# A convolution's last taps during attention: from multiplies and accumulating transfers to two GpSimd instructions per tap

## The chip, the cores and the metric

The kernel runs on one core of a Trainium2 chip. A core has five engines that run their own instruction streams and meet at semaphores: TensorE (PE in the profile, with its weight loads as PEld), VectorE (DVE), ScalarE (ACT), GpSimd (POOL) and SyncE (SP), which here only issues transfers. Transfers (DMA) run on 16 engines of their own; they are issued from SyncE's queue and from GpSimd's. The metric is the device time of one execution in microseconds (us), the median over several runs.

## The reference

Two layers of an encoder on a sequence of 1024 tokens with 1024 channels, then a final RMSNorm. In each layer a normalized input is projected once, and two things are computed from it side by side: attention with 8 heads, and a depthwise convolution of 31 taps on 512 channels. Both go through one output matrix; a gated feed-forward part follows.

```python
h = _rmsnorm(x, g_mix[l])
p = h @ w_in[l]
...                                   # queries, keys and values from p
y_attn = _mla_attention(q_nope, q_rope, k_nope, k_rope, v)
a, gt = jnp.split(p[..., o3:], 2, axis=-1)
u = a * jax.nn.sigmoid(gt)
u = _dwconv(u, w_dw_conv[l], b_dw_conv[l])          # 31 taps for each channel
u = jax.nn.silu(_layernorm(u, g_conv_ln[l], b_conv_ln[l]))
y = jnp.concatenate([y_attn, u], axis=-1) @ w_o[l]
x = x + y
...                                   # gated feed-forward part with a 3-tap convolution
```

The change concerns the line with `_dwconv`: for each channel c and time s it adds up 31 products w[t, c] * u[s + t - 15, c].

## The kernel before, in words

Channels lie on the 128 partitions and the 1024 tokens along the free dimension, so the convolution's 512 channels are four tiles of 128x1024, with j from 0 to 3. Its input tile is called gate in the profile (`u[j]`, which is made in place), its sum is `conv[j]`, and a tap's weight is a column of the parameter tile `par`, one number for each partition. A tap is a multiply of a shifted `u[j]` by that column, and an add into `conv[j]`.

The four sums are begun in the projections (`project`): ScalarE makes the middle tap with the bias, VectorE adds 12 to 16 taps for each j (L1734), and some taps go by ScalarE and an accumulating transfer (`tap_far`, L1740 and L1741). What is left, 50 taps in the first layer and 48 in the second, is called late and is done in `attention`.

Attention works in 64 steps, for 8 heads of 8 query tiles. In each step TensorE computes scores for two steps ahead (L1536, six matmuls of 512 columns), turns the probabilities of earlier tiles by eight transposes (L1565), and multiplies them with the values (L1588, four matmuls). VectorE finds the row maximum of the scores (L1538) and makes the low part of the turned probabilities (L1568), ScalarE takes the exponential (L1546) and casts the turned tiles (L1567).

The order of each engine's instructions is the order in which the program emits them; nothing reorders them. Work beside the steps is put on an agenda, a list of functions for each step, which run when that step has been emitted. GpSimd's stream in attention holds the following:

- the late taps, which the agenda spreads over the first 56 steps in proportion to planned costs (`LATE_COST`, `SIDE_TIME`);
- for every second head a multiply of the head pair's output `yt` by the inverse sums (L1614, agenda steps 23, 39 and 55), and five or four steps later the low half of that output (`ys`, L206), whose upper half is cast by ScalarE (L204);
- at step 55 four transfers that fetch parts of the output matrix (`wo`, L869). From step 58 on ScalarE negates each of them (L185) and GpSimd issues the accumulating transfer that completes it (L186);
- from step 60 on three adds that sum the four `conv[j]` into `lns` (L1762), for the layer norm's mean, which TensorE begins with (`lnp`, L1778).

A late tap has one of three kinds, in a pattern of five (`LATE_KINDS`), the first row for the first half of the taps and the second row for the second half:

- act: ScalarE multiplies in two halves (L1748, one half in each of two steps), and a transfer that GpSimd issues adds the product to `conv[j]` (L1756);
- pool: GpSimd multiplies by the tap, broadcast along the free dimension as a second tensor (L1751), and a transfer adds the product (L1756);
- both: GpSimd multiplies in the same way and adds by an instruction of its own (L1754).

The first layer has 30 taps of kind pool, 10 of kind both and 10 of kind act; the second has 29, 10 and 9. A tile for a product comes from a pool of 31 slots of 128x1024 that is shared with most other tiles (`blk`).

Of the kernel before, what the change touches and what calls it, by code (L numbers as in the profile page):

```python
# [12 lines left out]
AF = mybir.ActivationFunctionType  # L13
ALU = mybir.AluOpType
AX = mybir.AxisListType

T = 1024
# [55 lines left out]
ROW_LATE = {0: (6,)}  # L73
E = mybir.EngineType
MANUAL = [E.PE, E.DVE, E.Activation, E.Pool]
LATE_KINDS = (("pool", "both", "act", "pool", "act"), ("pool", "both", "pool", "pool", "pool"))
LATE_COST = {"act": 1.1, "pool": 3.5, "both": 4.8}
NEAR_TAPS = (12, 14, 16, 14)
NEAR_ORDER = (0, 1, 2, 3)
FAR_TOGETHER = 3  # L80
# [41 lines left out]
class Encoder:  # L122
# [1379 lines left out]
    def attention(self, l, u, conv, away, spill, kvs, loaded, ahead, wo, begun):  # L1502
# [147 lines left out]
        while any(rest.values()):  # L1650
            j = max((j for j in rest if rest[j]), key=lambda j: (all(j != e for e, _ in late[-2:]), len(rest[j]), -j))
            late.append((j, rest[j].pop(0)))
        kinds = [LATE_KINDS[2 * i // len(late)][i % 5] for i in range(len(late))]
        costs, taken = [LATE_COST[kind] for kind in kinds], set()
        for i, (j, t) in enumerate(late):
# [87 lines left out]
    def tap_late(self, l, j, t, u, y, kind):  # L1743
        lo, hi, s = self.span(t)
        p = self.blk(f"late{l}_{j}_{t}")
        if kind == "act":
            for a, b in ((lo, T // 2), (T // 2, hi)):
                self.nc.scalar.activation(out=p[:, a:b], in_=u[:, a + s:b + s], func=AF.Copy, scale=self.tap(l, j, t))  # L1748
                yield
        else:  # L1750
            self.nc.gpsimd.tensor_tensor(out=p[:, lo:hi], in0=u[:, lo + s:hi + s],  # L1751
                                         in1=self.tap(l, j, t).broadcast_to([128, hi - lo]), op=ALU.mult)
        if kind == "both":
            self.nc.gpsimd.tensor_tensor(out=y[:, lo:hi], in0=y[:, lo:hi], in1=p[:, lo:hi], op=ALU.add)  # L1754
        else:
            self.nc.gpsimd.dma_start(out=y[:, lo:hi], in_=p[:, lo:hi], accum_op=ALU.add)  # L1756

    def conv_total(self, l, conv, j):
        if j == 1:
# [137 lines left out]
```

## Time and profile before

| What | Value |
|---|---|
| median of 3 runs | 2277.29 us |
| lowest and highest | 2277.22 and 2278.43 us |
| the profiled execution's own span | 2274.7 us |
| TensorE busy in that span | 2267.6 us |
| GpSimd busy in that span | 782.9 us |
| attention, first layer | about 199 to 405 us |
| attention, second layer | about 1328 to 1534 us |

The span runs from the first to the last instruction of the profiled execution; the device time of a run has some 2.6 us around it. Times in views are in us from the span's start, means of one instruction in ns. In rows of the groups stands: line, engine, operation, out<-in by tile names, shapes, count, then busy time and mean of one, then the engine's idle time just before and what ended it. In rows of the timeline stands: start, duration, engine, line, operation, tiles, count, and in brackets the idle time before. A GpSimd instruction that follows a transfer's issue is shown from before that issue has ended, so its shown duration is longer by up to 0.3 us than that of one that follows another instruction.

### The profile page before, as it was taken

The page shows a single profiled execution, that of the slowest core. Times are in us where ns is not written, and L with a number is a line of the kernel's source. Part 1 is how long each engine was busy: PE and PEld are TensorE (multiplying, and loading weights), DVE is VectorE, ACT ScalarE, POOL GpSimd, SP SyncE. Part 2 cuts the span into 40 slices and gives each one's busy share as a digit, 9 for nine tenths or more (in the row PEclk, how much of TensorE's full clock was granted, in tenths as well). Part 3 has the DMA queues.
Part 4 walks back from the last instruction along what each step waited for, and adds up shares of the span by engine and source line. Part 5 has one row for each costly group of instructions (what it writes and reads, how often), then busy time and mean ns, then how long its engine had stood idle before and what let it go on. Part 6 is the DMA issues. An engine that isn't in the chain of part 4 may idle for free.

```text
span 2274.7 us, 30503 instructions
## 1 busy us (share of the span) xinstructions
PE 2267.6 (100%) x10682; PEld 1888.4 (83%) x10682; DVE 1724.7 (76%) x2299; ACT 1286.8 (57%) x2050; POOL 782.9 (34%) x812
## 2 busy tenths in 40 slices
PE   9999999999999999999999999999999999999999
PEld 8888888888888888888888888888888888888888
DVE  7989888768877776776559788886697777768765
ACT  5355877646655555544523468774475555555444
POOL 1222788532333333001412237873323333320032
PEclk9999999999999999999999999999999999999999
DMA  6889998856899998935968999967669999988356
GB/s 192 166 182 266 195 199 182 215 153 139 208 283 300 272 298 203 336 103 146 205 137 167 218 253 201 184 150 211 173 131 230 272 299 283 287 216 315 104 120 173
DMA packets 199145, 475.73 MB, mean 209 GB/s; under 512 B 27232, under 2 KB 35280, under 8 KB 198992
## 3 DMA queue, kind: packets, MB, share of 16 engines
q0 software_dynamic: 103136, 222.46, 48.7%
q1 hardware_dynamic: 95568, 250.80, 33.0%
q8 instruction: 84, 1.38, 0.2%
q14 instruction: 69, 0.57, 0.1%
q10 hardware_dynamic: 288, 0.53, 0.1%
HBM read 309.29 MB, written 80.40 MB: 171 GB/s over the span
## 4 chain that ended last, share of the span: by engine, by line
PE 96%; DVE 1%; DMA 1%; issue 1%; ACT 0%; POOL 0%; DVEq 0%; POOLq 0%; ACTq 0%; SPq 0%
PE p L1095 35%; PE pd L1283 18%; PE s L1536 8%; PE po L906 6%; PE o L1588 5%; PE t L1565 5%; PE pq L222 3%; PE pa L222 3%; PE pkv L222 2%; PE pg L222 2%; PE pg L541 2%; PE pn L222 1%; PE pv L1514 1%; PE pk L222 1%; PE pa L541 1%
## 5 line engine op out<-in xcount | busy, mean ns | idle before, releaser
L1095 PE MATMUL p<-b,w 128*128 128x512 f32 x3552 | 806.7, 389 | 0.1
L1095 PEld LDWEIGHTS p<-b,w 128*128 128x128 f32 x3552 | 666.4, 188 | 139.7 <-DVE w L1474 1.1
L1283 PE MATMUL pd<-ab,wd 128*128 128x512 f32 (+1 forms) x1920 | 422.2, 381 | 0.0
L1283 PEld LDWEIGHTS pd<-ab,wd 128*128 128x128 f32 x1920 | 350.8, 188 | 69.4 <-DVE ab L1474 0.4
L186 POOL DMA_DIRECT2D w<-wu x96 | 84.8, 886 | 359.6 <-ACT w L185 317.9
L1536 PE MATMUL s<-k,q 96*128 96x512 f32 x768 | 207.6, 405 | 0.0
L1568 DVE TENSOR_TENSOR pt<-t,pt 128x512 fp32r<-128x512 f32 x256 | 165.1, 686 | 53.1 <-ACT pt L1567 51.8
L1751 POOL TENSOR_TENSOR late<-gate,par 128x1014 f32<-128x1014 f32 (+12 forms) x79 | 171.7, 2173 | 18.7 <-DMA qrd<-qr 18.7
L1567 ACT CAST pt<-t 128x512 fp32r<-128x512 f32 x256 | 137.8, 589 | 66.5 <-PE t L1565 62.8
L1486 DVE SCALAR_TENSOR_TENSOR o<-zg,par,o 128x1023 f32<-128x1023 f32 x88 | 112.8, 1283 | 75.4 <-ACT o L1480 74.0
L186 POOL DMA_DIRECT2D w<-in_w_up x116 | 100.5, 867 | 199.6 <-ACT w L185 181.2
L1538 DVE TENSOR_REDUCE mx<-s 128x1 f32<-128x1024 f32 x128 | 155.8, 1217 | 0.6 <-PE s L1536 0.6
L1536 PEld LDWEIGHTS s<-k,q 96*128 96x128 f32 x768 | 135.4, 189 | 23.1
L1546 ACT ACTIVATE p<-s,mx 128x1024 f32<-128x1024 f32 x128 | 144.8, 1131 | 1.8 <-DVE mx L1538 1.8
L1734 DVE SCALAR_TENSOR_TENSOR conv<-gate,par,conv 128x1009 f32<-128x1009 f32 (+7 forms) x112 | 142.3, 1274 | 3.7 <-ACT conv L603 1.0
L1588 PE MATMUL o<-pt,v 128*128 128x512 f32 x512 | 140.8, 398 | 0.0
L869 POOL DMA_DIRECT2D wd<-in_w_down x44 | 32.8, 749 | 307.8 <-PE pd L1283 306.7
L1044 DVE TENSOR_TENSOR zg<-p,zg 128x512 f32<-128x512 f32 x88 | 60.6, 690 | 99.7 <-PE p L1095 92.5
L1472 ACT CAST ab<-ac 128x512 fp32r<-128x512 f32 x130 | 80.1, 617 | 98.2 <-DVE ac L1218 95.5
L185 ACT ACTIVATE w<-w 128x512 fp32r<-128x512 f32 x212 | 133.4, 629 | 3.0
L1565 PEld LDWEIGHTS t<-ident,p 128*128 128x128 f32 x1024 | 119.9, 141 | 18.2 <-ACT p L1546 0.4
L1565 PE MATMUL t<-ident,p 128*128 128x128 f32 x1024 | 133.0, 273 | 0.0
(2105 smaller groups left out, 4110.1 us busy)
## 6 DMA issues: line engine op xcount, KB each, us to landing
w<-in_w_up POOLq DMA_DIRECT2D x232, 256.0 KB, 7.1
wu<-in_w_up SPq DMA_DIRECT2D x88, 512.0 KB, 5.7
w<-wu POOLq DMA_DIRECT2D x96, 256.0 KB, 5.6
sd<-in_w_down SPq DMA_DIRECT2D x44, 512.0 KB, 9.6
ws<-sd SPq DMA_DIRECT2D x44, 512.0 KB, 6.6
wd<-in_w_down POOLq DMA_DIRECT2D x88, 256.0 KB, 5.4
act<-v SPq DMA_DIRECT2D x36, 512.0 KB, 5.4
ac<-act SPq DMA_DIRECT2D x72, 256.0 KB, 6.0
```

What stands on the lines that cost most here:

```text
L186: self.nc.gpsimd.dma_start(out=lo, in_=src, accum_op=ALU.add)
L222: nc.tensor.matmul(ps[:, HALVES[c]], w, x[:, HALVES[c]], start=(k == 0 and s == 0), stop=(k == n - 1 and s == 2))
L1095: nc.tensor.matmul(ps, w[p][:, k * 128:(k + 1) * 128], b[:, q], start=(i in (1, 5, 2) and k == 0 and t == 0), stop=(k == 3 and t == 2), sk ...
L1283: nc.tensor.matmul(ps[t, m][:, cs], w[i, j][p][:, m * 128:(m + 1) * 128], b[:, q, cs], start=(i in (1, 5, 2) and j == 0 and s == 0), stop= ...
L1536: nc.tensor.matmul(ps[:, cs], q[i][0:96, qs], k[j][0:96, cs], start=(s == 0), stop=(s == 2))
L1538: nc.vector.tensor_reduce(out=mx, in_=ps, op=ALU.max, axis=AX.X, negate=True)
L1546: nc.scalar.activation(out=p, in_=ps, func=AF.Exp, bias=mx, accum_out=st["sums"][:, qt:qt + 1])
L1565: nc.tensor.transpose(tp[:, i, qi * 128:(qi + 1) * 128], st["p"][2 * qp + qi][:, kt * 128:(kt + 1) * 128], self.ident)
L1568: nc.vector.tensor_tensor(out=lo, in0=tp, in1=hi.bitcast(F32), op=ALU.subtract)
L1588: nc.tensor.matmul(po, v[2 * c + i][:, h // 2, e, :], pt[s][:, i, :], start=(c == 0 and i == 0 and s == 0), stop=(c == 3 and i == 1 and s ...
L1734: self.nc.vector.scalar_tensor_tensor(out=y[:, lo:hi], in0=u[:, lo + s:hi + s], scalar=self.tap(l, j, t), in1=y[:, lo:hi], op0=ALU.mult, o ...
L1751: self.nc.gpsimd.tensor_tensor(out=p[:, lo:hi], in0=u[:, lo + s:hi + s], in1=self.tap(l, j, t).broadcast_to([128, hi - lo]), op=ALU.mult)
```

## The change: two kinds of late taps in place of three

The kinds both and pool become one: GpSimd multiplies with the tap as a scalar operand (one tensor operand and a pointer to one number for each partition) and adds the product to `conv[j]` itself. Only the act taps still end in a transfer. The pattern keeps the act taps at the same places of the list, and the planned costs are replaced, so some taps move by a step on the agenda.

```diff
-LATE_KINDS = (("pool", "both", "act", "pool", "act"), ("pool", "both", "pool", "pool", "pool"))
-LATE_COST = {"act": 1.1, "pool": 3.5, "both": 4.8}
+LATE_KINDS = (("pool", "pool", "act", "pool", "act"), ("pool", "pool", "pool", "pool", "pool"))
+LATE_COST = {"act": 1.1, "pool": 3.6}
@@ def tap_late(self, l, j, t, u, y, kind):
         lo, hi, s = self.span(t)
         p = self.blk(f"late{l}_{j}_{t}")
-        if kind == "act":
-            for a, b in ((lo, T // 2), (T // 2, hi)):
-                self.nc.scalar.activation(out=p[:, a:b], in_=u[:, a + s:b + s], func=AF.Copy, scale=self.tap(l, j, t))
-                yield
-        else:
-            self.nc.gpsimd.tensor_tensor(out=p[:, lo:hi], in0=u[:, lo + s:hi + s],
-                                         in1=self.tap(l, j, t).broadcast_to([128, hi - lo]), op=ALU.mult)
-        if kind == "both":
+        if kind == "pool":
+            self.nc.gpsimd.tensor_scalar(out=p[:, lo:hi], in0=u[:, lo + s:hi + s], scalar1=self.tap(l, j, t), scalar2=None, op0=ALU.mult)
             self.nc.gpsimd.tensor_tensor(out=y[:, lo:hi], in0=y[:, lo:hi], in1=p[:, lo:hi], op=ALU.add)
-        else:
-            self.nc.gpsimd.dma_start(out=y[:, lo:hi], in_=p[:, lo:hi], accum_op=ALU.add)
+            return
+        for a, b in ((lo, T // 2), (T // 2, hi)):
+            self.nc.scalar.activation(out=p[:, a:b], in_=u[:, a + s:b + s], func=AF.Copy, scale=self.tap(l, j, t))
+            yield
+        self.nc.gpsimd.dma_start(out=y[:, lo:hi], in_=p[:, lo:hi], accum_op=ALU.add)
```

In the changed file the multiply is L1747, the add L1748, the transfer of an act tap L1753, the sums into `lns` L1759. The streams of TensorE, VectorE and SyncE hold the same instructions in the same order as before. ScalarE's holds the same instructions, with some of the late halves one step earlier.

## The prediction

> **What bounds the kernel now.** I read the page's totals first, then the busy time in windows over the two attention stages, since all that changes lies there, and then the chain of waits.
>
> ```profile
> span 2274.7 us, 30503 instructions
> PE 2267.6 (100%) x10682; PEld 1888.4 (83%) x10682; DVE 1724.7 (76%) x2299; ACT 1286.8 (57%) x2050; POOL 782.9 (34%) x812
> PE 96%; DVE 1%; DMA 1%; issue 1%; ACT 0%; POOL 0%; DVEq 0%; POOLq 0%; ACTq 0%; SPq 0%
> ```
>
> ```profile
> 199.00:405.00 206.00, 206.00 (x1153) 173.77 (x1152) 174.62 (x226) 166.08 (x307) 155.99 (x104) 1.00 0.92 204
> 1328.00:1534.00 206.00, 206.00 (x1154) 173.76 (x1153) 172.44 (x226) 163.98 (x301) 152.19 (x102) 1.00 0.89 197
> ```
>
> The window rows give length, then busy time of PE, PEld, DVE, ACT and POOL, granted clock, DMA share and GB/s. TensorE is busy in every microsecond of both stages at full clock. A busy PE could still hide pauses, so the pieces of the chain have to show its pace. Here are one step and the hand-over to the layer norm:
>
> ```profile
> 357.50 1.38 PE s L1536 x6
> 358.89 0.94 PE o L1588 x4
> 359.82 0.87 PE t L1565 x8
> ...
> 416.97 1.37 PE po_e L906 x6
> 418.34 0.93 PE lnp L1778 x4
> ```
>
> A step is 1.38 + 0.94 + 0.87 = 3.19 us, and 62 such steps fill the 198 us from 206 to 404 us: the chain runs along TensorE without a gap, to the first matmul of the layer norm at 418.34 us, which follows the piece before it at once (416.97 + 1.37). GpSimd is on none of it. So a lighter GpSimd or DMA gains nothing here; GpSimd matters only where it comes too late for somebody that TensorE waits for. The question is when its stream reaches its deadlines.
>
> **What a late tap costs before.**
>
> ```profile
> L1751 POOL TENSOR_TENSOR late<-gate,par 128x1014 f32<-128x1014 f32 (+12 forms) x79 | 171.7, 2173 | 18.7 <-DMA qrd<-qr 18.7
> L1756 POOL DMA_DIRECT2D conv<-late x78 | 69.1, 927 | 74.6 <-ACT late L1748 21.2 <-DMA conv<-late 16.0 <-POOL late L1751 15.4
> L1754 POOL TENSOR_TENSOR conv<-conv,late 128x1016 f32<-128x1016 f32 (+11 forms) x20 | 47.6, 2379 | 1.6
> ```
>
> ```profile
> 348.63 2.19 POOL L1751 TENSOR_TENSOR late<-gate,par 128x1011 f32<-128x1011 f32 x1
> 351.12 0.89 POOL L1756 DMA_DIRECT2D conv<-late  x1 [0.30 <-POOL late L1751]
> 351.73 2.18 POOL L1751 TENSOR_TENSOR late<-gate,par 128x1011 f32<-128x1011 f32 x1
> 353.99 2.37 POOL L1754 TENSOR_TENSOR conv<-conv,late 128x1011 f32<-128x1011 f32 x1
> 356.32 2.39 POOL L206 TENSOR_TENSOR ys_3l<-yt,ys_3h 128x1024 fp32r<-128x1024 f32 x1
> 358.68 1.87 POOL L1751 TENSOR_TENSOR late<-gate,par 128x1010 f32<-128x1010 f32 x1
> ```
>
> From start to start, multiply and transfer take 3.10 us (348.63 to 351.73), and the add occupies 2.33 us (353.99 to 356.32). The multiply alone is 1.87 us where no issue overlaps it, with 0.08 us before an add. Kind pool costs 3.1 us, kind both about 4.3 us.
>
> **The change, part by part.**
>
> *The scalar multiply*, 79 times in place of the 171.7 us of L1751. No GpSimd instruction with one tensor operand of this size is in the trace. Upper end: 2.38 us, the add with two full operands. Lower end: 1.05 us, which ScalarE needs for a cast of a whole tile (L204, below). The broadcast multiply already shows that a second operand that stays in place saves 0.5 us (1.87 against 2.37). I take 1.2 us, half of the add, since half of the tensor reads remain; it is an estimate.
>
> *The add* replaces 59 issues of transfers (30 + 29 taps): 59 x 2.38 = 140 us more, 59 x 0.9 = 53 us fewer. With 79 x (2.17 - 1.2) = 77 us saved, GpSimd's busy time goes from 782.9 to about 793 us. A tap is then 1.2 + 0.08 + 2.33 = 3.61 us, against 3.1 and 4.3 before, on average (59 x 3.1 + 20 x 4.3) / 79 = 3.4. So the stream is about as long.
>
> *The 59 transfers*, some 0.5 MB each, leave GpSimd's queue, and with them waits for earlier ones into the same sum. TensorE waits for no transfer in these stages, so I cost this at nothing.
>
> *New waits.* GpSimd's add after an act tap on the same `conv[j]` must wait for that transfer's landing, and all of GpSimd's stream stands behind it: taps, `yt`, `ys`, `wo`. There are seven such adds in layer 0, all but two in the first half. What paces that half today is ScalarE, whose act taps GpSimd issues in order (timeline of GpSimd and of ScalarE, then the landings of the late transfers from 199 to 300 us):
>
> ```profile
> 290.08 0.89 POOL L1756 DMA_DIRECT2D conv<-late  x1 [5.34 <-DMA conv<-late]
> ...
> 296.14 1.21 POOL L1756 DMA_DIRECT2D conv<-late  x1
> 296.74 2.51 POOL L1751 TENSOR_TENSOR late<-gate,par 128x1014 f32<-128x1014 f32 x1
> ```
>
> ```profile
> 285.42 0.72 ACT L1748 ACTIVATE late<-gate,par 128x503 f32<-128x503 f32 x1
> ...
> 349.48 1.05 ACT L204 CAST ys_3h<-yt 128x1024 fp32r<-128x1024 f32 x1
> ...
> 392.49 1.07 ACT L1567 CAST pt<-t 128x512 fp32r<-128x512 f32 x2 [1.06 <-PE t L1565]
> ...
> 394.55 0.64 ACT L185 ACTIVATE wo<-wo 128x512 fp32r<-128x512 f32 x1
> ...
> 398.40 1.05 ACT L204 CAST ys_5h<-yt 128x1024 fp32r<-128x1024 f32 x1
> ...
> 1410.92 0.72 ACT L1748 ACTIVATE late<-gate,par 128x503 f32<-128x503 f32 x1
> ...
> 1522.96 0.64 ACT L185 ACTIVATE wo<-wo 128x512 fp32r<-128x512 f32 x1
> ```
>
> ```profile
> DMA to landing us min/median/max: 4.6/7.5/13.1
> ```
>
> The last act tap ends at 285.42 + 0.72 = 286.1 us, and keeps its place on the agenda. Up to there GpSimd has 16 taps (57.8 us) and 9 issues (8.0 us) from 199.1 us on: 265 us without a wait, so 21 us of waiting are covered. Seven landings of 7.5 us, each partly under the multiply and whatever stands between, fit into that.
>
> **Where the stream arrives.** The deadlines stand at the end of each attention:
>
> ```profile
> 384.27 2.46 POOL L869 DMA_DIRECT2D wo<-in_w_o  x4
> 386.50 2.65 POOL L1614 TENSOR_TENSOR yt<-yt,rb 128x1024 f32<-128x1024 f32 x1
> ...
> 1479.04 2.40 POOL L206 TENSOR_TENSOR ys_3l<-yt,ys_3h 128x1024 fp32r<-128x1024 f32 x1 [3.12 <-ACT ys_3h L204]
> ...
> 1508.10 2.45 POOL L869 DMA_DIRECT2D wo<-in_w_o  x4
> ```
>
> ```profile
> wo<-in_w_o POOLq DMA_DIRECT2D x32, 256.0 KB, 8.0
> ```
>
> The last row is the transfers from 380 to 440 us, with the median time to landing. ScalarE negates the first `wo` at 394.55 us, in its one stream with the casts that TensorE needs. With 8.0 us to land, the issue must come by 386.5 us, 2.3 us later than today; in layer 1 by 1522.96 - 8.0 = 1515.0, 6.9 us later. About 1 us more hides in ScalarE's own waiting for TensorE (1.06 us at 392.49). `yt` has more: it ends at 389.2 and is read at 398.40.
>
> Layer 0 after the change: tap 26 done at about 286, `yt` 2.35 and one issue 0.89 to 289.3. From there 16 taps (57.8), one `ys` and one `yt` (4.7) to 351.8; `ys_3l` may start from 350.5 on, when its cast has ended. Then 2.35 and 8 taps (28.9): the `wo` issue comes at 383.1, before 386.5. If the landings hold GpSimd until 296.7, where it stands today, it comes at 390.5, 3 us too late after the 1 us of cover; with no wait at all, at 381.8.
>
> Layer 1: the last act tap ends at 1411.6; an issue, a tap and `yt` (6.9) bring 1418.5; 15 taps, `ys` and `yt` (58.9) 1477.4, before the 1479.04 at which `ys_3l` could start; then 2.4 + 28.9: 1510.3, before 1515.0.
>
> The sum is nothing: no us is added to TensorE's chain and none is taken from it. The profiled execution's 2274.7 us stay, and with the 2.6 us around the span the median stays at 2277.3.
>
> The point that is not seen is the scalar multiply. With d us more than 1.2 for each, the issue comes 24d later in layer 0 and 23d in layer 1, against slacks of 3.4 + 1.0 and 4.7 + 1.0: nothing up to d = 0.18, and 47d - 10.1 beyond 0.25. At 2.38 us this is 45 us, a time of 2323; at 1.05 us nothing, as `ys_3l` waits for its cast.
>
> **A rule beside the row.** The add's 2.37 us for 1011 elements is the row. The Trainium skill, "GPSIMD Engine Reference", 3.1 Elementwise — side-by-side cycle accounting, puts two-operand work at about 2.6 cycles an element since both operands share a read port, and its best loop at 1.8 cycles; at its 1.2 GHz that is an estimate of 2.2 and 1.5 us, so the row agrees for the add, and no row shows a one-operand loop. By its 1.5 us the sum above would be about 4 us, not 0; its 4.1 Engine selection, which calls one-input work roughly line-rate, would leave it at 0.
>
> **The rivals.**
>
> *The loop, not the reads, paces the scalar multiply*: halfway between half an add and the broadcast multiply, 1.54 us, d = 0.34. Then 47 x 0.34 - 10.1 = 5.9 us, 2283. For it: dropping the second moving operand saved 0.5 us, not half. Against it: with the operand gone altogether a read goes too. It passes 0.2% from 1.51 us on. It is the mechanism of the 1.8 cycles above.
>
> *Slower: the scalar form is no faster than the broadcast one* (the change would not do what it says): 1.87 us, d = 0.67, 47 x 0.67 - 10.1 = 21 us, 2298. For it: nothing in the trace shows such a form. Against it: it has one tensor operand fewer.
>
> *Slower: the landings block GpSimd.* At the longest landing of 13.1 us, seven waits are 7 x 5.6 = 39 us longer; 21 are covered, 18 push layer 0's issue to 401, 14 us too late: 2291. It decides from some 26 us of waits. Against it: late transfers fall from 40 to 10 in a layer where the DMA share is 0.92.
>
> *Faster: something behind attention gains from fewer transfers.* Between 481 and 560 us TensorE does wait a little:
>
> ```profile
> PEld p L1095 <- DVE w L1474: 0.7, 2, 0.5
> ```
>
> That is 0.7 us, 2276.6 without it; no stage shows 4.6 us that could be won.
>
> *GpSimd's busier adds slow VectorE?* The low part of the turned tiles, with GpSimd idle (207 to 219 us) and full (326 to 384):
>
> ```profile
> L1568 DVE TENSOR_TENSOR pt<-t,pt x6: 681/681/691, 211.0 to 217.9; 128x512 fp32r<-128x512 f32 x6
> ```
>
> ```profile
> L1568 DVE TENSOR_TENSOR pt<-t,pt x37: 680/691/693, 325.7 to 383.5; 128x512 fp32r<-128x512 f32 x37
> ```
>
> 10 ns on 681, and GpSimd is full there already: nothing.
>
> **How the numbers follow.** 0.2% is 4.6 us, about what a measurement of this kernel tells from no change. Chances: forecast 0.69; loop-paced multiply 0.10, half of it on each side of 0.2%; no faster than the broadcast 0.11; landings 0.07; faster 0.03, of which 0.01 within 0.2%. So faster 0.02, same 0.75, slower 0.23. The predicted time is 2277.3. The range goes down to 2275.5 (the 0.7 us and the runs' spread of 1.2) and up to 2285, which takes in the loop-paced multiply and small landing waits and leaves out the two large rivals.
>
> **What would show it.** Right: L1747 at about 1.2 us a piece and L1748 at 2.35 to 2.4, GpSimd's busy time near 793 us, 19 transfers at L1753, `wo` issued by 386.5 and 1515 us, and the step at 3.19 us throughout, with the layer norm's first matmul near 418.3 us. Wrong: L1747 above 1.5 us, or long waits of L1748 for transfers, then ScalarE's L185 waiting for `wo` and a TensorE gap at step 58.

## The result: 4.0% slower, and the profile after

The changed kernel takes 2367.25 us (median of 4 runs, 2365.41 to 2374.57) against 2277.86 us before on the same chip: a ratio of 1.0398, 95% interval 1.0383 to 1.0413. The prediction was 2277.3 us with a range up to 2285, so it was wrong, by 89 us. The profiled execution took 2374.57 us, with a span of 2372.8 us, 98.1 us more than the 2274.7 us of before. (The runs list spans some 1.8 us below their times; the 2.6 us around the span given above is the median less the span of one execution. Nothing in the argument hangs on it.)

First the totals of the changed kernel's page (the third line is the chain that ended last, by engine), and its two groups of instructions for a GpSimd tap:

```profile
span 2372.8 us, 30424 instructions
PE 2297.6 (97%) x10682; PEld 1905.4 (80%) x10682; DVE 1736.9 (73%) x2299; ACT 1290.1 (54%) x2050; POOL 939.5 (40%) x812
PE 80%; POOL 10%; DVE 4%; DMA 2%; issue 2%; ACT 1%; POOLq 0%; DVEq 0%; SPq 0%; ACTq 0%
...
L1747 POOL TENSOR_SCALAR late<-gate,par 128x1014 f32<-128x1014 f32 (+12 forms) x79 | 229.8, 2909 | 19.1 <-DMA qrd<-qr 19.1
L1748 POOL TENSOR_TENSOR conv<-conv,late 128x1014 f32<-128x1014 f32 (+12 forms) x79 | 186.7, 2363 | 8.6 <-DMA conv<-late 2.1
```

TensorE is still busy for 97% of the span, but it is no longer nearly the whole chain: its share fell from 96% to 80%, and GpSimd holds 10%, where it held 0%. The add costs what was predicted (2.36 us). The scalar multiply takes 2.91 us on average, more than the broadcast multiply that it replaces (2.17) and more than the add with its two tensors. GpSimd's busy time rose by 156.6 us.

Here are GpSimd's timelines around the deadlines that the prediction named, in the first layer, before and after (start, length, engine, line, operation, tiles):

```profile
293.79 2.71 POOL L1614 TENSOR_TENSOR yt<-yt,rb 128x1024 f32<-128x1024 f32 x1
...
340.12 2.70 POOL L1614 TENSOR_TENSOR yt<-yt,rb 128x1024 f32<-128x1024 f32 x1
```

```profile
298.06 2.38 POOL L1614 TENSOR_TENSOR yt<-yt,rb 128x1024 f32<-128x1024 f32 x1
...
366.60 2.34 POOL L1614 TENSOR_TENSOR yt<-yt,rb 128x1024 f32<-128x1024 f32 x1
...
392.23 2.81 POOL L1747 TENSOR_SCALAR late<-gate,par 128x1010 f32<-128x1010 f32 x1
395.13 2.36 POOL L1748 TENSOR_TENSOR conv<-conv,late 128x1010 f32<-128x1010 f32 x1
397.45 2.84 POOL L1747 TENSOR_SCALAR late<-gate,par 128x1010 f32<-128x1010 f32 x1
...
433.95 2.24 POOL L869 DMA_DIRECT2D wo<-in_w_o  x4
```

A tap takes 397.45 - 392.23 = 5.22 us from start to start, 2.90 us of them up to the start of its add, where 3.1 us (pool) and 4.3 us (both) stood before. The lateness builds up: 4 us at the first `yt`, 26 us at the second, and the `wo` issue comes at 433.95 instead of 384.27, 50 us late.

Who waits for it is in the waits (engine, tile and line, what it waited for: us in total, times, longest), and what that does to TensorE in the busy time in windows of the first layer (length, busy time of PE, PEld, DVE, ACT and POOL, granted clock, DMA share, GB/s):

```profile
ACT wo L185 <- DMA wo<-in_w_o: 27.8, 8, 8.0
...
ACT p L1546 <- POOL conv L1748: 22.2, 5, 8.5
...
ACT ys_3h L204 <- POOL yt L1614: 14.6, 2, 8.8
```

```profile
300.00:400.00 100.00, 84.52 (x437) 69.44 (x436) 65.06 (x82) 58.10 (x104) 98.58 (x40) 0.91 0.29 61
...
400.00:420.00 20.00, 11.71 (x53) 9.61 (x52) 8.83 (x11) 7.42 (x13) 19.67 (x9) 0.74 0.04 13
```

ScalarE, which serves TensorE in every step, stands for `yt`, for `wo`, and for the exponential's tile `p`: every fourth `p` takes a slot of the shared pool (`blk`), and waits there until GpSimd's add has read out the product that held it. Of the 27.8 us for `wo`, 12.7 us stood there before the change too; the other two waits are new. GpSimd is busy for 98.6 of 100 us, TensorE for 84.5.

VectorE, which works beside GpSimd, is not what makes the multiply long, as far as these windows show: it is busy for 65.06 of 100 us in the first window and for 8.83 of 20 us in the second, and the scalar multiplies that follow an add take 2.81 to 2.84 us in both. The layer norm's first matmul shows what each layer loses (operation and tiles, shortest, median and longest in ns, first and last start):

```profile
L1778 PE MATMUL lnp<-lns0h,ones_r x2: 392/394/397, 418.2 to 418.6; 128*128 128x512 f32 x2
L1778 PE MATMUL lnp<-lns1h,ones_r x2: 392/394/397, 1546.6 to 1547.1; 128*128 128x512 f32 x2
```

```profile
L1775 PE MATMUL lnp<-lns0h,ones_r x2: 392/394/397, 467.1 to 467.5; 128*128 128x512 f32 x2
L1775 PE MATMUL lnp<-lns1h,ones_r x2: 392/394/397, 1644.7 to 1645.1; 128*128 128x512 f32 x2
```

It starts 48.9 us later in the first layer and 98.1 us later in the second: the whole loss lies in the two attentions, about half in each.

### The profile page after: what moved, and what is told of

The parts are those of the page before. It is cut to its first block, busy times and chain, and to the rows that moved or that the text cites. A ratio compares the mean times of both kernels' runs of the same rounds, so it can differ in the third digit from the quotient of the medians.

```text
span 2372.8 us, 30424 instructions
## 1 busy us (share of the span) xinstructions
PE 2297.6 (97%) x10682; PEld 1905.4 (80%) x10682; DVE 1736.9 (73%) x2299; ACT 1290.1 (54%) x2050; POOL 939.5 (40%) x812
## 4 chain that ended last, share of the span: by engine, by line
PE 80%; POOL 10%; DVE 4%; DMA 2%; issue 2%; ACT 1%; POOLq 0%; DVEq 0%; SPq 0%; ACTq 0%
PE p L1095 32%; PE pd L1283 18%; PE po L906 7%; POOL late L1747 5%; POOL conv L1748 4%; PE s L1536 4%; PE o L1588 3%; PE t L1565 2%; PE pa L222 2%; PE pg L222 2%; DVE conv L1734 2%; PE pg L541 1%; PE pq L222 1%; PE pn L222 1%; PE pv L1514 1%
## 5 line engine op out<-in xcount | busy, mean ns | idle before, releaser
L1747 POOL TENSOR_SCALAR late<-gate,par 128x1014 f32<-128x1014 f32 (+12 forms) x79 | 229.8, 2909 | 19.1 <-DMA qrd<-qr 19.1
L1568 DVE TENSOR_TENSOR pt<-t,pt 128x512 fp32r<-128x512 f32 x256 | 166.4, 687 | 94.2 <-ACT pt L1567 82.0
L1536 PE MATMUL s<-k,q 96*128 96x512 f32 x768 | 216.8, 419 | 0.1
L1748 POOL TENSOR_TENSOR conv<-conv,late 128x1014 f32<-128x1014 f32 (+12 forms) x79 | 186.7, 2363 | 8.6 <-DMA conv<-late 2.1
L1565 PE MATMUL t<-ident,p 128*128 128x128 f32 x1024 | 142.4, 282 | 47.2 <-ACT p L1546 26.2
L1565 PEld LDWEIGHTS t<-ident,p 128*128 128x128 f32 x1024 | 125.2, 146 | 69.9 <-ACT p L1546 27.7
L186 POOL DMA_DIRECT2D w<-in_w_up x116 | 98.6, 851 | 199.4 <-ACT w L185 178.2
L1588 PE MATMUL o<-pt,v 128*128 128x512 f32 x512 | 147.5, 412 | 19.3 <-ACT pt L1567 17.2
L1536 PEld LDWEIGHTS s<-k,q 96*128 96x128 f32 x768 | 141.4, 197 | 25.6 <-ACT p L1546 1.0
L185 ACT ACTIVATE w<-w 128x512 fp32r<-128x512 f32 x212 | 133.5, 630 | 3.4 <-DMA w<-in_w_up 0.4
L1588 PEld LDWEIGHTS o<-pt,v 128*128 128x128 f32 x512 | 98.8, 197 | 45.0 <-ACT pt L1567 18.5
```

Source lines behind the costliest of these rows:

```text
L186: self.nc.gpsimd.dma_start(out=lo, in_=src, accum_op=ALU.add)
L1536: nc.tensor.matmul(ps[:, cs], q[i][0:96, qs], k[j][0:96, cs], start=(s == 0), stop=(s == 2))
L1565: nc.tensor.transpose(tp[:, i, qi * 128:(qi + 1) * 128], st["p"][2 * qp + qi][:, kt * 128:(kt + 1) * 128], self.ident)
L1568: nc.vector.tensor_tensor(out=lo, in0=tp, in1=hi.bitcast(F32), op=ALU.subtract)
L1588: nc.tensor.matmul(po, v[2 * c + i][:, h // 2, e, :], pt[s][:, i, :], start=(c == 0 and i == 0 and s == 0), stop=(c == 3 and i == 1 and s ...
L1747: self.nc.gpsimd.tensor_scalar(out=p[:, lo:hi], in0=u[:, lo + s:hi + s], scalar1=self.tap(l, j, t), scalar2=None, op0=ALU.mult)
```

## The experiments

Two theories stood against each other at first. By the one, the multiply is longer than taken, and GpSimd's stream comes too late. By the other, the own adds are what costs: they put waits and work into GpSimd's stream that transfers carried before.

**The own adds alone.** The multiply goes back to the broadcast form; all else is as in the changed kernel.

```diff
-            self.nc.gpsimd.tensor_scalar(out=p[:, lo:hi], in0=u[:, lo + s:hi + s], scalar1=self.tap(l, j, t), scalar2=None, op0=ALU.mult)
+            self.nc.gpsimd.tensor_tensor(out=p[:, lo:hi], in0=u[:, lo + s:hi + s],
+                                         in1=self.tap(l, j, t).broadcast_to([128, hi - lo]), op=ALU.mult)
```

> The changed kernel with only the multiply undone: GpSimd multiplies by the broadcast tap again and adds each of its products itself. Theory A (the scalar multiply, 2.82 us in place of 1.87, makes GpSimd's stream too long): a tap is 1.87 + 0.08 + 2.33 = 4.28 us in place of 5.23, the first layer's stream of 40 taps is 38 us shorter, the fetch of wo is issued at 394 to 400 us in place of 432, 8 to 13 us too late in each layer, so 2290 to 2302 us. Theory B (the 59 additional adds on GpSimd and what waits for them are the cause, whatever the multiply): 2340 us or more. L1747 stands at 1.87 to 2.2 us either way.

Measured: 2305.9 us, ratio 1.0123 (1.0108 to 1.0138), some 4 us above the first theory's range and far under the second's. Taking back the multiply's form wins 61 of the 89 us. The other 28 us come with taps of 1.88 + 0.08 + 2.33 = 4.29 us against 3.4 before on average. In the first layer `wo` is issued 17 us late (384.27 before):

```profile
401.35 2.22 POOL L869 DMA_DIRECT2D wo<-in_w_o  x4
```

**The scalar multiply alone.** The kernel before, with the transfers kept and only the multiply changed.

```diff
-            self.nc.gpsimd.tensor_tensor(out=p[:, lo:hi], in0=u[:, lo + s:hi + s],
-                                         in1=self.tap(l, j, t).broadcast_to([128, hi - lo]), op=ALU.mult)
+            self.nc.gpsimd.tensor_scalar(out=p[:, lo:hi], in0=u[:, lo + s:hi + s], scalar1=self.tap(l, j, t), scalar2=None, op0=ALU.mult)
```

> The kernel before with only the multiply changed to the scalar form; kinds, planned costs and transfers stay. Theory A: every GpSimd tap is 0.95 us longer; from 296.7 us on, where the stream of before has no waits of its own left, 24 taps add 23 us, so the first layer's fetch of wo comes at 407 us, some 20 us too late, the second layer's some 16: 2300 to 2320 us. Theory B: no added adds, so 2277 to 2283 us.

Measured: 2325.86 us, ratio 1.0211 (1.0194 to 1.0228), a little above the range that the first theory gave. The scalar form loses time with the transfers in place too. Each part of the change is slower by itself, the multiply by 48 us and the adds by 28; together they make 89, which is 13 more than the sum. Both lengthen the same stream, so a slack that covers a part of each by itself is there only once for the two. That this is the whole of the 13 us is not shown.

**Fewer taps at the end.** GpSimd's taps 29 and 30, eight in each layer at the end of its stream, are left out of the changed kernel and of the computation.

```diff
+        if kind == "pool" and t >= 29:
+            return
         if kind == "pool":
```

> The changed kernel without the last two GpSimd taps of each of the four sums in each layer (taps 29 and 30 are left out of the convolution). Both theories: 8 x 5.23 = 42 us less GpSimd work in each layer, so the fetch of wo comes at about 390 us in layer 0 and the time falls to 2277 to 2288 us; the granted clock is back at 1.00 throughout. A third theory C, that the lowered clock (0.985 in the mean) costs by itself whatever GpSimd does: the clock stays lowered and the time stays above 2300.

Measured: 2323.21 us, ratio 1.02 (1.0184 to 1.0215). This missed: eight taps of 5.2 us are 42 us in each layer, and in sum only 44 us went. The rows of ScalarE and of GpSimd in the first layer say why:

```profile
299.74 1.06 ACT L204 CAST ys_1h<-yt 128x1024 fp32r<-128x1024 f32 x1 [1.66 <-POOL yt L1614]
...
305.86 1.11 ACT L1546 ACTIVATE p<-s,mx 128x1024 f32<-128x1024 f32 x1 [2.04 <-POOL conv L1750]
...
339.69 1.11 ACT L1546 ACTIVATE p<-s,mx 128x1024 f32<-128x1024 f32 x1 [8.50 <-POOL conv L1750]
...
368.20 1.04 ACT L204 CAST ys_3h<-yt 128x1024 fp32r<-128x1024 f32 x1 [6.66 <-POOL yt L1614]
```

```profile
397.41 2.24 POOL L869 DMA_DIRECT2D wo<-in_w_o  x4 [5.88 <-PE s L1536]
```

`wo` is in time now, and GpSimd even waits 5.88 us for TensorE before it. But the cast of `ys` at 368.20 stands 18.7 us behind its place of before (349.48), and the layer norm of this layer starts 19.4 us late, at 437.6. ScalarE's four waits up to this cast sum to 18.9 us: 8.3 us for `yt` (1.66 and 6.66), and 10.5 us for slots that `p` takes (2.04 and 8.50; L1750 is the add in this kernel). So there are deadlines in the middle of the attention that bind by themselves when the one at the end is relieved, and the larger part of this lateness comes from slots of the shared pool.

The third theory's time fits here, with a granted clock of 0.992. The last run below rules it out: there the scalar form is kept, the clock stands at 0.999 and nothing is lost.

**The operation by itself.** In the kernel before, 45 GpSimd instructions on a tile of their own run in the first layer's down projection, three of each form and width, in place (the 1014 columns onto the same tile shifted by 10).

```diff
+            for n in (1014, 504, 252):
+                o, i, y = x[:, 0:n], x[:, T - n:T], x[:, 512:512 + n] if n < 512 else x[:, 0:n]
...
+                    g.tensor_scalar(out=o, in0=i, scalar1=w, scalar2=None, op0=ALU.mult)
...
+                    g.tensor_scalar(out=o, in0=i, scalar1=0.5, scalar2=None, op0=ALU.mult)
...
+                    g.tensor_copy(out=o, in_=i)
...
+                    g.tensor_tensor(out=o, in0=i, in1=w.broadcast_to([128, n]), op=ALU.mult)
...
+                    g.tensor_tensor(out=o, in0=i, in1=y, op=ALU.add)
```

> The kernel before with 45 GpSimd instructions on a tile of its own, put where GpSimd is idle for over 100 us in the first layer's down projection: three each of the multiply by a pointer scalar, the multiply by a constant, a copy, the multiply by a broadcast tensor and the add of two tensors, on 1014, 504 and 252 columns. Theory A: 2.8, then 1.87 and 2.35 us for the pointer scalar, the broadcast and the add at 1014 columns. If a constant scalar is as slow as the pointer, the tensor-scalar form itself is slow and not the fetch of the scalar; if it takes about 1.2 us, the pointer is. A copy near 1 us would show that one tensor operand alone does run faster than two. Durations in proportion to the columns mean a cost by element, not by instruction. The time itself stays at 2277 to 2280 us.

Its groups of 1014 and of 252 columns (busy time, mean of one in ns; L1367 takes the weight from memory, L1369 a constant, L1371 copies, L1373 multiplies by the broadcast weight, L1375 adds):

```profile
L1367 POOL TENSOR_SCALAR probe<-probe,par 128x1014 f32<-128x1014 f32 x3 | 11.3, 3781 | 0.3
L1369 POOL TENSOR_SCALAR probe<-probe 128x1014 f32<-128x1014 f32 x3 | 8.3, 2758 | 0.3
L1375 POOL TENSOR_TENSOR probe<-probe 128x1014 f32<-128x1014 f32 x3 | 6.9, 2312 | 0.2
L1373 POOL TENSOR_TENSOR probe<-probe,par 128x1014 f32<-128x1014 f32 x3 | 6.6, 2203 | 0.2
L1369 POOL TENSOR_SCALAR probe<-probe 128x252 f32<-128x252 f32 x3 | 4.0, 1339 | 0.3
L1371 POOL COPY probe<-probe 128x1014 f32<-128x1014 f32 x3 | 3.8, 1267 | 0.2
...
L1373 POOL TENSOR_TENSOR probe<-probe,par 128x252 f32<-128x252 f32 x3 | 2.8, 934 | 0.2
```

One tensor operand is quick in a copy (1.27 us) and slow with a scalar: 2.76 us with a constant, more than two tensors take (2.31). The mean with the weight, 3.78 us, covers 5.04 us for the first and 2.84 and 3.46 for the others, so it says no more than 2.84 or above. At 252 columns the scalar form with a constant still takes 1.34 us, where the broadcast one takes 0.93: a quarter of the columns brings it down to a half only.

The probe's own time, 2288.1 us (ratio 1.0046), lies above the 2277 to 2280 us that were expected, and it says nothing of the taps: the probe slows VectorE, for which TensorE waits 7.0 us in the down projection and did not wait before. Here are VectorE's instructions on two tensors from 930 to 1020 us, before and with the probe:

```profile
L1474 DVE TENSOR_TENSOR ab<-ac,ab 128x512 fp32r<-128x512 f32 x37 | 25.5, 690 | 2.8
```

```profile
L1492 DVE TENSOR_TENSOR ab<-ac,ab 128x512 fp32r<-128x512 f32 x31 | 31.4, 1013 | 1.0
```

So the probe's durations may be longer than they would be without VectorE's instructions beside them, and the next two runs weigh more. In attention VectorE shows no such slowing: its L1568 has a median of 683 ns before and 691 after the change.

**A copy in the place of the multiply.** The taps' weights are left out of the computation; instruction count, tiles and order are those of the changed kernel.

```diff
-            self.nc.gpsimd.tensor_scalar(out=p[:, lo:hi], in0=u[:, lo + s:hi + s], scalar1=self.tap(l, j, t), scalar2=None, op0=ALU.mult)
+            self.nc.gpsimd.tensor_copy(out=p[:, lo:hi], in_=u[:, lo + s:hi + s])
```

> The changed kernel with the multiply replaced by a plain copy of the same elements on GpSimd, so that the weights of these taps are left out of the computation. In the probe the copy took 3.92 us for three at 1014 elements, some 1.3 us each: close to the 1.2 us that the prediction took for the multiply. Theory A (the multiply's own time is what failed; the rest of the sum stands): a tap is 1.3 + 0.08 + 2.33 = 3.7 us, GpSimd keeps its deadlines or misses them by a few us, and the time is 2277 to 2283. Theory B (something else in the change costs too: waits of GpSimd's own adds for transfers, the add against TensorE's other suppliers): 2290 or more.

Measured: 2278.47 us, ratio 1.0004 (0.9995 to 1.0013). The group of the copies, the `wo` issue and the window of the first attention:

```profile
L1747 POOL COPY late<-gate 128x1014 f32<-128x1014 f32 (+12 forms) x79 | 87.5, 1107 | 18.5 <-DMA qrd<-qr 18.5
L1748 POOL TENSOR_TENSOR conv<-conv,late 128x1014 f32<-128x1014 f32 (+12 forms) x79 | 189.0, 2393 | 18.0 <-DMA conv<-late 11.9
```

```profile
380.04 2.21 POOL L869 DMA_DIRECT2D wo<-in_w_o  x4
```

```profile
199.00:405.00 206.00, 206.00 (x1153) 173.77 (x1152) 174.16 (x226) 166.09 (x306) 165.40 (x104) 1.00 0.52 128
```

With a first instruction of 1.11 us, near the 1.2 us of the prediction's sum, that sum holds in all its other terms as long as nothing comes too late: own adds, fewer transfers (the DMA share falls from 0.92 to 0.52), waits for landings (11.9 us, covered), a full TensorE.

**A constant in the place of the weight.** The weights are left out here too; the instruction stays in its scalar form.

```diff
-scalar1=self.tap(l, j, t)
+scalar1=0.5
```

> The changed kernel with the constant 0.5 in the place of the tap's weight, so that the weights of these taps are left out of the computation; the instruction is the same but reads no scalar from memory. Theory A (the scalar form itself is slow on GpSimd, wherever the scalar comes from): the multiply stays at 2.8 us and the time at 2360 to 2375. Rival C (reading the scalar operand from memory is what costs; in the probe the form with it took 3.78 us against 2.76): 1.8 to 2.2 us each, and 2300 to 2325.

Measured: 2360.65 us, ratio 1.0367 (1.0346 to 1.0387), and this group:

```profile
L1747 POOL TENSOR_SCALAR late<-gate 128x1014 f32<-128x1014 f32 (+12 forms) x79 | 223.9, 2834 | 19.3 <-DMA qrd<-qr 19.3
```

2.83 us in place of 2.91 on average: the scalar form is slow wherever its scalar comes from.

**As many taps fewer, but spread.** Of the changed kernel's taps, those of the fourth tile (j = 3) from 23 on are left out: eight in each layer, as many as at the end before, one in four.

```diff
+        if kind == "pool" and j == 3 and t >= 23:
+            return
         if kind == "pool":
```

> The changed kernel without GpSimd's taps of the fourth convolution block from tap 23 on: 8 taps left out in layer 0 and 7 or 8 in layer 1, as many as in the kernel that left out the last eight of each layer and stood at 2323, but every fourth one instead of the end of the stream. Theory A1 (GpSimd has deadlines all along the attention, the casts of yt and the reuse of tiles, so that what counts is the pace of its stream): 2285 to 2305, clearly under 2323. Theory A2 (one deadline at the end counts, as the prediction has it, and the mid-stream waits of the shortened kernel were something else): the same number of taps is worth the same, 2318 to 2328.

Measured: 2293.43 us, ratio 1.0066 (1.005 to 1.0083), against 2323.21 with the same number left out at the end. Taken out evenly, they bring 74 us of the 84 that two times 42 us are worth; at the end 44. (Here a tap that is left out still takes its product tile from the pool, though no instruction uses it; in the run above it takes none. What this does to `p`'s waits is not separated from the pace.) In the first layer the cast of `ys` is in time again, and `wo` is the one that is late:

```profile
348.75 1.05 ACT L204 CAST ys_3h<-yt 128x1024 fp32r<-128x1024 f32 x1
399.11 0.63 ACT L185 ACTIVATE wo<-wo 128x512 fp32r<-128x512 f32 x1 [5.09 <-DMA wo<-in_w_o]
```

**Every second one fewer.** The same with the taps of the third tile (j = 2) too, 29 in all.

```diff
+        if kind == "pool" and j in (2, 3) and t >= 23:
+            return
         if kind == "pool":
```

> As the kernel before it, with the third and the fourth convolution block's taps of GpSimd from 23 on left out: 15 in layer 0, 14 in layer 1, every second one. The stream is then 25 taps of 5.2 us, 131 us, against 40 of 3.4 us, 136 us, before the change. Theory A1: 2277 to 2281, no measurable change against the kernel before. If the scalar form harmed anything beside GpSimd's own pace (VectorE, the granted clock of TensorE by itself), 2285 or more would remain.

Measured: 2277.61 us, ratio 1.0002 (0.9993 to 1.0012). With scalar multiplies of 2.84 us (their median), 25 taps in a layer cost nothing; 40 cost 49 us in the first layer of the changed kernel. What counts is the length of the stream, not the form as such.

## Why the prediction was wrong, point by point

- **The step that failed: "I take 1.2 us, half of the add, since half of the tensor reads remain".** The multiply took 2.91 us on average, 2.83 in the middle. The upper end of 2.38 us was broken too. It rested on a reason that excluded more than it could: that an instruction with one tensor operand fewer can't be slower than the add. No row of the trace had that form; the nearest rows bounded what operands cost, not what an operation costs. The copy shows that the reasoning on operands was sound for a copy (1.04 us, ScalarE's 1.05 beside it), so the operation was the unknown.
- **The rival that named the mechanism** ("the scalar form is no faster than the broadcast one") had 0.11 and 2298 us: the side was right, the size a quarter of the loss.
- **The second failure, the slope.** With the measured length d is 2.83 - 1.2 = 1.63, and 47d - 10.1 gives 66 us: 2344 instead of 2367. The 47 counts the taps of the second half only, since "21 us of waiting are covered" in the first. That cover is soon used up: 16 taps of 5.23 us and 8.0 us of issues are 91.7 us, where 87 us lie up to the last act tap. The first `yt` ends at 300.4 us, and the prediction's stream had it at 286 + 2.35 = 288.4. These 12 us ride on to the end: the prediction's 383.1 us for the `wo` issue and 24 times 1.63 make 422.2 us, and it came at 433.95. Four kernels that differ in this instruction alone show the slope:

| First instruction of a tap | median, us | time, us | above before, us |
|---|---|---|---|
| copy | 1.04 | 2278.47 | 1 |
| broadcast multiply | 1.88 | 2305.9 | 28 |
| scalar multiply, constant | 2.76 | 2360.65 | 83 |
| scalar multiply, weight | 2.83 | 2367.25 | 89 |

Their medians are in these rows (shortest, median, longest, in ns; the kernels in the table's order):

```profile
L1747 POOL COPY late<-gate x79: 1019/1039/1367, 198.8 to 1505.7; 128x1014 f32<-128x1014 f32 x8, 128x1013 f32<-128x1013 f32 x8, 128x1012 f32<-128x1012 f32 x8, 128x1011 f32<-128x1011 f32 x8
```

```profile
L1747 POOL TENSOR_TENSOR late<-gate,par x79: 1861/1877/2507, 199.5 to 1538.5; 128x1014 f32<-128x1014 f32 x8, 128x1013 f32<-128x1013 f32 x8, 128x1012 f32<-128x1012 f32 x8, 128x1011 f32<-128x1011 f32 x8
```

```profile
L1747 POOL TENSOR_SCALAR late<-gate x79: 2735/2757/3397, 200.6 to 1595.8; 128x1014 f32<-128x1014 f32 x8, 128x1013 f32<-128x1013 f32 x8, 128x1012 f32<-128x1012 f32 x8, 128x1011 f32<-128x1011 f32 x8
```

```profile
L1747 POOL TENSOR_SCALAR late<-gate,par x79: 2809/2832/3675, 199.9 to 1606.5; 128x1014 f32<-128x1014 f32 x8, 128x1013 f32<-128x1013 f32 x8, 128x1012 f32<-128x1012 f32 x8, 128x1011 f32<-128x1011 f32 x8
```

From the broadcast to the scalar multiply it is 61 us for 0.95 us, 64 us for each us: between the 47 of the prediction and all 79 taps.

- **The deadlines.** That `wo` binds at the end was right: its negation by ScalarE starts at 437.06 us after the change instead of 394.55, and the layer norm 48.9 us late. That "`yt` has more" slack holds for the last `yt` alone, the one that was looked at. The `yt` before it is 26 us late, and its cast 19.5 (ScalarE's rows below; 349.48 before). In the changed kernel the end is later still and decides; where the end was relieved, the middle kept 19 us of the first layer. One kind of deadline the prediction does not name at all: the slots of the shared pool. From 190 to 480 us of the changed kernel ScalarE waits 21.0 us for adds of GpSimd that have to free a slot (15.2 for `p`, 5.8 for `pt`), more than the 7.9 us for `wo` and the 7.5 us for `yt` (5.9 and 1.6). Its waits in this stretch are below.

```profile
368.97 1.04 ACT L204 CAST ys_3h<-yt 128x1024 fp32r<-128x1024 f32 x1 [5.87 <-POOL yt L1614]
...
437.06 0.63 ACT L185 ACTIVATE wo<-wo 128x512 fp32r<-128x512 f32 x1 [7.94 <-DMA wo<-in_w_o]
```

```profile
ACT p L1546 <- POOL conv L1748: 15.2, 3, 8.5
...
ACT wo L185 <- DMA wo<-in_w_o: 7.9, 1, 7.9
...
ACT ys_3h L204 <- POOL yt L1614: 5.9, 1, 5.9
...
ACT pt L1567 <- POOL conv L1748: 5.8, 2, 4.1
```

- **What held:** TensorE as the bound of before, the add at 2.36 us, 19 transfers at L1753, the removal of 59 transfers as worth nothing, waits for landings that stay covered, VectorE hardly slowed in attention (L1568 at 691 ns against 683). The copy puts these together to 1.0004. "ScalarE's L185 waiting for `wo`" was named as the sign of a wrong forecast, and it did grow, from 12.7 to 27.8 us over both layers.
- **The pages.** The Trainium skill, "GPSIMD Engine Reference", 4.1 Engine selection, calls one-input work roughly line-rate. The copy's 1.04 us for 1014 elements, about one ns each, fits that; the scalar form's 2.83 us doesn't, and the measurement decides. The same page of the Trainium skill, in 3.1 Elementwise — side-by-side cycle accounting, has a best loop of 1.8 cycles, which the prediction made an estimate of 1.5 us; the scalar form doesn't reach that either.

Open is why the scalar form is so long. The probe tells the operation from the operands, but not what in it takes the time, nor why the first with the weight took 5.04 us there.

## What to carry to other kernels

A form of instruction that no row shows is unknown as an operation, not only in its operands: bound it by the slowest row of that engine or above, and where the sum has little slack, measure it first with a few instances beside other work. On this chip's GpSimd a multiply by one number for each partition is cheaper as a tensor-tensor instruction with the number broadcast (1.9 us at 1014 columns) than as a scalar operand (2.8 us). An engine off the critical path has several deadlines, and the moment at which it frees a shared tile is one of them; take its arrival at each of them, with its lag carried on from one to the next, and not at the last one alone.

## What the runs showed of the hardware that was not expected

- GpSimd's scalar form is slower than its two-tensor forms: 2.83 us against 1.88 (broadcast multiply) and 2.36 (add), a copy taking 1.04; in the probe at 252 columns 1.34 us (with a constant) against 0.93.
- GpSimd's work can lengthen VectorE's: with the probe beside them, VectorE's instructions `ab<-ac,ab` on two tensors took 1013 ns on average against 690 before, and 1.49 us beside GpSimd's copies and 2.47 us beside its adds (rows below). VectorE's L1568 in attention stayed at 691 against 683.
- TensorE's granted clock falls around its long pauses: 0.74 from 400 to 420 us of the changed kernel, in which one pause lasts 8.29 us (row below), 1.00 from 380 to 400 us, where the pauses sum to 2.04 us, and 1.00 throughout the attention of the kernel with the copy. TensorE's busy time rose from 2267.6 to 2297.6 us for the same 10682 matmuls; the other 68 of the 98 us are pauses. No run tells how much of these 30 us would have been pause anyway, at full clock, with GpSimd setting the pace. The Trainium skill, "TensorE: Matmul & The Clock Gate", What's actually happening, has the clock halved after an idle window of some 3.4 us; the windows agree in kind, and no view here shows the single switch.

```profile
414.42 1.54 PE L1565 MATMUL t<-ident,p 128*128 128x128 f32 x6 [8.29 <-ACT p L1546]
```

```profile
958.36 1.49 DVE L1492 TENSOR_TENSOR ab<-ac,ab 128x512 fp32r<-128x512 f32 x1
...
969.50 2.47 DVE L1492 TENSOR_TENSOR ab<-ac,ab 128x512 fp32r<-128x512 f32 x1
```
